# Sums of one-addend norms as transposes with VectorE adding columns, the last norm's spread in one bank, and the second input tile issued on ScalarE's queue

## The chip, the cores and the metric

The kernel runs on one core of one Trainium2 chip. The metric is device time in microseconds (us) of one execution; lower is better. Five engines work side by side and meet at semaphores: TensorE (PE in the profile; its weight loads are PEld), VectorE (DVE), ScalarE (ACT), GpSimd (POOL) and SyncE (SP), which here only issues DMAs. ScalarE issues some DMAs as well. Each engine works through its own list of instructions in order. Every queue of DMAs is served by the same 16 DMA engines.

## The reference

One encoder layer over 1024 tokens of width 1024, in float32:

```
hn   = rmsnorm(x, norm_mix)
proj = hn @ w_in                          # 1024 x 2304
o_a  = window_gqa_sink(qa, ka, va, sink)  # 8 query heads, 2 key heads, |i-j| <= 128, rotary
o_b  = neighbourhood_attention(qb, kb, vb, rpb)   # 8 heads, 2-D window 8 x 16, learned bias
mix  = concat(rmsnorm(o_a, norm_a), rmsnorm(o_b, norm_b))
h    = x + mix @ w_out
hn   = rmsnorm(h, norm_ffn)
h    = h + (silu(conv3(hn @ w_gate)) * (hn @ w_up)) @ w_down      # 1024 x 2816 between
out  = rmsnorm(h, norm_final)
```

with `rmsnorm(x, g) = x * rsqrt(mean(x * x) + 1e-6) * g`, the mean taken over the features of one token. There are five such norms.

## The kernel before

Activations are kept transposed: 128 features in the partitions, tokens along the row, so a tile is 128 x 1024 (or 128 x 512 for one half of the tokens). Every matrix product is float32 made of three passes: each operand is split into a rounded high part (ScalarE, a Copy) and the remainder (VectorE, a subtraction), and TensorE adds high x high, high x low and low x high into one PSUM bank (`block`, lines 167 to 170, and `group`, lines 881 to 885). PSUM has eight banks, taken under the tags pj, o, s and pt, two each.

The program runs in five stages: (1) the head, where the input x and the first three column tiles of w_in are loaded and split and six banks are filled (lines 85 to 164 and 576 to 660); (2) attention, with the remaining projections as filler between its steps (to line 826); (3) the end of w_out (lines 827 to 965); (4) the gated MLP's first half; (5) the product with w_down and the final norm (from line 1147). The order of TensorE's instructions is written out by hand (`manual_schedule`, line 127). The other engines' lists are put in order by a planner with its own model of costs; `pin` and `behind` fix some places in it. So an edit in one place can move instructions of other places in the lists of ScalarE, VectorE, GpSimd and SyncE.

*The head.* `load_x(k)` loads input tile k, `load_first_w(m, ks)` the k-tiles `ks` of column tile m (m = 0, 1, 2). SyncE issues x0's first half, then w at k = 0, w at k = 1, both halves of x1, w at k = 2 and 3, x2, x3, w at k = 4 to 7, x4 to x7; ScalarE issues the small parameters and x0's second half. `split_x` and `split_first_w` split them in the same order, and `add_square` adds up the squares of x over the eight tiles on VectorE. TensorE then goes over k, per k over two token halves and three column tiles. Behind the x tiles SyncE issues the constants, the rotary table, the next column tiles' weights (`fetch_w`, line 154, into `raw`, two buffers) and the tables of the learned bias (`bias_tiles`, line 435, into `rr`, one buffer). GpSimd builds a bias tile from `rr` (lines 443 and 444), and only then may the next `rr` be loaded. ScalarE and VectorE split `raw` (lines 160 and 161).

*A norm.* The squares are added over the feature tiles on VectorE until one 128 x 512 tile (the addend) stands for a token half; what is left is a sum over the partitions. `inverse_narrow` does this on TensorE: for each 128 tokens the addend is the stationary operand and a column of ones (each 1/1024) the moving one, which leaves one column of PSUM per 128 tokens (line 199); ScalarE takes the root (line 202), VectorE the reciprocal (line 203). `widen` then spreads the four columns over all partitions with four transposes of a broadcast column (line 210) into a bank. It is called twice in the head (addend `acc`), twice for norm_a (`narrow_a`, `wide_a`), twice for norm_b (`vb2`, line 843), once for each half of norm_ffn (lines 953 and 1099), and for the final norm once for the second token half (line 1368) and once for each quarter of the first half (lines 1385 and 1390), each with two addends `parts[..., 2]` and `parts[..., 3]`.

*The final norm.* `finish` (line 1299) calls `widen` twice, into two banks: one is read by VectorE, which scales six of the eight output tiles (line 1309), the other is copied to SBUF by ScalarE (line 1303), for GpSimd, which scales the other two (line 1307). Each tile's store is issued after it (line 1310), for the last quarter in turn by SyncE and ScalarE.

In the head TensorE's order is: the last k-tiles of column tile 0, four blocks with the two sums in their middle (line 646), two blocks of column tile 1, the two spreads (line 649), then two more blocks of column tile 1 and four of column tile 2. ScalarE copies the spread to `rstd1`, and VectorE multiplies the six banks with it (line 216).

Of the kernel before, what the change touches and what calls it, by code (L numbers as in the profile page):

```python
# [53 lines left out]
def hybrid_layer(tc, xT, w_in, w_out, w_gate, w_up, w_down, small, sink, rpb, consts, rope, out):  # L54
    nc = tc.nc
    with ExitStack() as ctx:
        pool = lambda name, bufs, **kw: ctx.enter_context(tc.tile_pool(name=name, bufs=bufs, **kw))
        cpool = pool("const", 1)
# [29 lines left out]
        def load_x(k, part=slice(0, S), queue=nc.sync):  # L88
            pin(queue.dma_start(xts[k][:, part], xT[k, :, part]))
# [11 lines left out]
        def load_first_w(m, ks):  # L101
            raw, at = head[ks.start // 4][m][0], slice(ks.start % 4, ks.start % 4 + ks.stop - ks.start)
            pin(nc.sync.dma_start(raw[:, at], w_in[m, :, ks, :]))

        steps = [slice(0, 1), slice(1, 2), slice(2, 4), slice(4, 8)]
        load_x(0, tsl(0))
        nc.scalar.dma_start(par[:, 0:C_SINK], small)
        load_x(0, tsl(1), nc.scalar)
        for m in range(3):
            load_first_w(m, steps[0])  # L110
        for m in range(3):
            load_first_w(m, steps[1])
        load_x(1, tsl(0))
        load_x(1, tsl(1))
        for m in range(3):
            load_first_w(m, steps[2])
        for k in (2, 3):
            load_x(k)
        for m in range(3):
            load_first_w(m, steps[3])  # L120
# [73 lines left out]
        def inverse_narrow(sqs, dim, tag, n=4):  # L194

            ps = bank("ss", tag)
            for i, sq in enumerate(sqs):
                for c in range(n):
                    nc.tensor.matmul(ps[:, c:c + 1], sq[:, c * 128:(c + 1) * 128], ones[:, 0:1], start=c == 0 and i == 0,
                                     stop=i == len(sqs) - 1, skip_group_check=True)  # L200
            v = cpool.tile([128, 4], F32, name="v4", tag="v4", bufs=4)
            nc.scalar.activation(v[:, 0:n], ps[:, 0:n], AF.Sqrt, bias=eps, scale=float(D) / dim)
            nc.vector.reciprocal(v[:, 0:n], v[:, 0:n])
            return v

        def widen(v, tag, n=4):

            wide = bank("sw", tag)
            for c in range(n):
                nc.tensor.transpose(wide[:, c * 128:(c + 1) * 128], v[:, c:c + 1].to_broadcast([128, 128]), ident)  # L210
            return wide
# [375 lines left out]
        def split_first_w(m, ks):  # L587
            raw, hi, lo = (t[:, ks.start % 4:ks.start % 4 + ks.stop - ks.start] for t in head[ks.start // 4][m])
            pin(nc.scalar.activation(hi, raw, AF.Copy))
            pin(nc.vector.tensor_tensor(lo, raw, f32(hi), op=ALU.subtract))  # L590
            first[m].w += [(hi[:, j], lo[:, j]) for j in range(ks.stop - ks.start)]

        def add_square(t, acc):
            s2 = tmp("sq")
            pin(nc.scalar.activation(s2, t, AF.Square))
            if acc is not None:
                pin(nc.vector.tensor_tensor(s2, s2, acc, op=ALU.add))
            return s2
# [10 lines left out]
            split_first_w(m, steps[1])  # L609
        for h in range(2):  # L610
            split_x(1, tsl(h))
        for m in range(3):
            split_first_w(m, steps[2])
        acc = add_square(xts[0], None)
        for k in range(2, KT):
            split_x(k)
            if k == 3:
                for m in range(3):
                    split_first_w(m, steps[3])
# [226 lines left out]
        for h in range(2):  # L846
            wide = widen(vb2[h], "pt")
# [96 lines left out]
        for h in range(2):  # L944
            for d in range(KT):
                if h == 0 and d + 2 < KT:
                    wo.append(load_wo(d + 2, fpool))
                ps = bank("pj", ("o", "s", "pj")[(h * KT + d) % 3])
# [3 lines left out]
                if h == 1 and d == 1:  # L952
                    v = inverse_narrow([total[0]], D, "pt")
# [5 lines left out]
                if h == 1 and d == 2:  # L959
                    wide = widen(v, "pt")  # L960
# [138 lines left out]
        v = inverse_narrow([total[1]], D, "pt")  # L1099
        units[1].p2()  # L1100
        wide = widen(v, "pt")
# [174 lines left out]
        sq, todo, vs = {}, [], {}  # L1276
# [21 lines left out]

        def finish(h, v, cols=whole, split=False):
            n = (cols.stop - cols.start) // 128  # L1300
            wide, again = widen(v, "pt", n), widen(v, "pt", n)
            copy = half("wide")
            nc.scalar.activation(copy[:, cols], again[:, 0:128 * n], AF.Copy)  # L1303
            for i, d in enumerate([d for d in range(KT) if d not in APART] + list(APART)):
                x = at_res(d, h, cols)
                if d in APART:
                    nc.gpsimd.tensor_tensor(x, x, copy[:, cols], op=ALU.mult)  # L1307
                else:
                    nc.vector.scalar_tensor_tensor(x, x, col(C_NFIN + d), wide[:, 0:128 * n], op0=ALU.mult, op1=ALU.mult)
                (nc.scalar if split and i % 2 else nc.sync).dma_start(out[d, :, h * HALF + cols.start:h * HALF + cols.stop], x)  # L1310
# [12 lines left out]
        def leave_quarter(j, ps, cols):  # L1323

            x = at_res(j + NP, 0, cols)
            add(j + NP, 0, ps, cols)
            s2 = parts[cols.start, j] = half("s2")[:, cols]
            nc.scalar.activation(s2, x, AF.Square)
            if j + NP < KT - 1:
                nc.vector.tensor_tensor(s2, s2, sq[0][:, cols], op=ALU.add)  # L1330

        tags = lambda j, y: ("s", "s", "pt", "pt")[j] if y else ("pj", "pj", "o", "o")[j]
        banks = {}
# [2 lines left out]
        for i, (p, j, c) in enumerate(order):  # L1336
# [4 lines left out]
            f, n = PARTS[c]  # L1341
# [4 lines left out]
            ps = banks[p, j]  # L1346
# [139 lines left out]
```

## Time and profile before

| | |
|---|---|
| Median of 3 runs | 1087.44 us (1087.1 to 1087.69) |
| Profiled execution | 1088.62 us |
| Its span, first to last instruction | 1086.8 us |
| Instructions | 14983 |
| Mean granted TensorE clock | 0.997 of full speed |
| Moved by DMA | 144.94 MB |

The profiled execution's own time stands 1.18 us above the median of the runs, and 1.8 us lie around its span. In the profile's rows `L199` is line 199 of the kernel before; a row of the timeline has start, duration, engine, line, operation, output <- inputs, shape and count, and in brackets how long the engine was idle before it and what released it. A float32 matmul with a one-column moving operand leaves two records.

### The profile page before, as it was taken

The numbers are of one execution on the slowest core, as the hardware profiler recorded it, in microseconds if no ns is written. First come the engines' busy times: TensorE is split into PE (matmuls) and PEld (weight loads), VectorE is DVE, ScalarE is ACT, GpSimd is POOL, SyncE is SP. The second block draws the span as 40 slices with busy tenths as digits, with TensorE's granted clock in tenths as the row PEclk, the third lists the DMA queues.
The fourth block names the chain that finished last, engine by engine and source line by source line (L and its number), as shares of the span: only waits on it lengthen the run. The fifth ranks groups of instructions, "written<-read, shape, count | busy, mean of one in ns | idle before, by whom it ended". The sixth has DMA issues, their size and how long they took to land.

```text
span 1086.8 us, 14983 instructions
## 1 busy us (share of the span) xinstructions
PE 1070.2 (98%) x5144; PEld 895.0 (82%) x5144; DVE 860.1 (79%) x1570; ACT 554.5 (51%) x1047; POOL 105.0 (10%) x188
## 2 busy tenths in 40 slices
PE   8999999999999999999999999999999999999997
PEld 7888888888888888887788888888888888888887
DVE  6789787667788688899998877877887867897764
ACT  7457676556676545545434334342433645444451
POOL 0223332222232100000000000000000000000001
PEclk9999999999999999999999999999999999999998
DMA  8223022232225147214342222323322788867644
GB/s 275 73 73 88 30 68 59 78 77 78 78 68 161 65 137 249 88 39 157 134 146 107 107 107 97 120 95 111 111 88 97 244 297 295 272 214 241 227 129 155
DMA packets 69084, 144.94 MB, mean 133 GB/s; under 512 B 8208, under 2 KB 19600, under 8 KB 69008
## 3 DMA queue, kind: packets, MB, share of 16 engines
q1 hardware_dynamic: 58784, 118.43, 34.6%
q10 hardware_dynamic: 10224, 25.56, 6.2%
q8 instruction: 40, 0.66, 0.3%
q14 instruction: 36, 0.29, 0.1%
HBM read 103.58 MB, written 28.57 MB: 122 GB/s over the span
## 4 chain that ended last, share of the span: by engine, by line
PE 88%; DVE 8%; ACT 2%; DMA 1%; issue 1%; SPq 0%; POOL 0%; DVEq 0%; ACTq 0%; POOLq 0%
PE pj L168 7%; PE pj L169 7%; PE pj L170 7%; PE dn L883 6%; PE dn L885 6%; PE dn L884 6%; PE z L885 5%; PE z L884 5%; PE z L883 5%; PE s L344 3%; PE x L883 3%; PE x L884 3%; PE x L885 3%; PE y L885 3%; PE y L884 3%; PE y L883 3%
## 5 line engine op out<-in xcount | busy, mean ns | idle before, releaser
L872 ACT ACTIVATE whi<-ws 128x512 fp32r<-128x512 f32 (+1 forms) x100 | 60.3, 623 | 127.8 <-DVE ws L990 80.5
L883 PE MATMUL dn<-xd,whi 128*128 128x512 f32 (+1 forms) x330 | 124.1, 376 | 0.0
L885 PE MATMUL dn<-xd,wlo 128*128 128x512 f32 (+1 forms) x330 | 123.7, 375 | 0.0
L884 PE MATMUL dn<-xd,whi 128*128 128x512 f32 (+1 forms) x330 | 123.7, 375 | 0.0
L168 PE MATMUL pj<-xgh,whi 128*128 128x512 f32 x248 | 104.4, 421 | 1.0 <-ACT xgh L584 1.0
L885 PE MATMUL z<-hg,wlo 128*128 128x512 f32 x264 | 103.0, 390 | 0.7 <-DVE wlo L873 0.7
L883 PE MATMUL z<-hg,whi 128*128 128x512 f32 x264 | 102.9, 390 | 0.0
L884 PE MATMUL z<-hg,whi 128*128 128x512 f32 x264 | 102.7, 389 | 0.0
L370 ACT ACTIVATE p<-p,nm 128x385 f32<-128x385 f32 (+3 forms) x128 | 75.1, 587 | 50.4 <-DVE nm L366 49.3
L169 PE MATMUL pj<-xgl,whi 128*128 128x512 f32 x248 | 97.5, 393 | 0.9 <-DVE xgl L585 0.8
L170 PE MATMUL pj<-xgh,wlo 128*128 128x512 f32 x248 | 97.6, 394 | 0.0
L374 POOL TENSOR_SCALAR p<-p,sm 128x384 f32<-128x384 f32 (+1 forms) x128 | 74.9, 598 | 219.3 <-DVE sm L372 204.7
L873 DVE TENSOR_TENSOR wlo<-raw,whi 128x512 fp32r<-128x512 f32 (+1 forms) x102 | 66.4, 671 | 26.6 <-ACT whi L872 26.4
L872 ACT ACTIVATE whi<-raw 128x512 fp32r<-128x512 f32 (+1 forms) x102 | 60.6, 612 | 45.2 <-DMA raw<-in_w_down_dram 20.0
L873 DVE TENSOR_TENSOR wlo<-ws,whi 128x512 fp32r<-128x512 f32 (+1 forms) x100 | 66.9, 681 | 21.0 <-ACT whi L872 20.8
L380 DVE TENSOR_TENSOR pl<-pt,ph 128x384 fp32r<-128x384 f32 (+2 forms) x108 | 63.3, 589 | 24.3 <-ACT ph L379 23.0
L1307 POOL TENSOR_TENSOR h<-h,wide 128x256 f32<-128x256 f32 (+1 forms) x6 | 5.4, 924 | 709.9 <-ACT wide L1303 709.9
L379 ACT ACTIVATE ph<-pt 128x384 fp32r<-128x384 f32 (+2 forms) x108 | 55.2, 514 | 32.2 <-PE pt L479 25.1
L885 PEld LDWEIGHTS dn<-xd,wlo 128*128 128x128 f32 x330 | 62.1, 188 | 11.3
L884 PEld LDWEIGHTS dn<-xd,whi 128*128 128x128 f32 x330 | 62.1, 188 | 11.1
L883 PEld LDWEIGHTS dn<-xd,whi 128*128 128x128 f32 x330 | 62.1, 188 | 11.1
L1198 ACT ACTIVATE xd<-xd 128x512 fp32r<-128x512 f32 x77 | 47.5, 626 | 44.0 <-DMA xd<-x 43.2
(220 smaller groups left out, 2671.2 us busy)
## 6 DMA issues: line engine op xcount, KB each, us to landing
xd<-x SPq DMA_DIRECT2D x77, 256.0 KB, 4.6
raw<-in_w_down_dram SPq DMA_DIRECT2D x72, 256.0 KB, 3.6
raw<-in_w_gate_dram SPq DMA_DIRECT2D x22, 512.0 KB, 3.4
raw<-in_w_up_dram SPq DMA_DIRECT2D x22, 512.0 KB, 3.8
x<-c ACTq DMA_DIRECT2D x22, 512.0 KB, 3.5
raw<-in_w_in_dram SPq DMA_DIRECT2D x30, 256.0 KB, 2.9
raw<-in_w_down_dram SPq DMA_DIRECT2D x36, 192.0 KB, 3.8
x<-t ACTq DMA_DIRECT2D x11, 512.0 KB, 2.6
```

Of the source, the lines that this page charges most:

```text
L168: nc.tensor.matmul(ps, w[0], x[0][:, tsl(h)], start=first, stop=False)
L169: nc.tensor.matmul(ps, w[0], x[1][:, tsl(h)], start=False, stop=False)
L170: nc.tensor.matmul(ps, w[1], x[0][:, tsl(h)], start=False, stop=last)
L370: nc.scalar.activation(p[:, j, 0:e], p[:, j, 0:e], AF.Exp, bias=nm, scale=-1.0, accum_out=sm[:, j:j + 1])
L374: nc.gpsimd.tensor_scalar(p[:, i, 0:m], p[:, i, 0:m], sm[:, i:i + 1], 1.0, op0=ALU.mult, op1=ALU.mult)
L379: nc.scalar.activation(ph[:, 0:n], ps[:, 0:n], AF.Copy)
L380: nc.vector.tensor_tensor(pl[:, 0:n], ps[:, 0:n], f32(ph[:, 0:n]), op=ALU.subtract)
L872: nc.scalar.activation(hi, src, AF.Copy)
L873: nc.vector.tensor_tensor(lo, src, f32(hi[:, :, :]), op=ALU.subtract)
L883: nc.tensor.matmul(ps, w[0], x[0], start=first and i == 0, stop=False, skip_group_check=True)
L884: nc.tensor.matmul(ps, w[0], x[1], start=False, stop=False, skip_group_check=True)
L885: nc.tensor.matmul(ps, w[1], x[0], start=False, stop=last and i == len(ws) - 1, skip_group_check=True)
```

## The change

Four edits:

1. `inverse_narrow` has two ways. With one addend, TensorE transposes it in 128-column pieces into a PSUM bank (one pass each, tokens now in the partitions), VectorE sums each piece along the row with one `tensor_reduce`, and the root reads its result from SBUF with the scale 1/dim. With two addends it is as before.
2. `finish` calls `widen` once, and VectorE and ScalarE read the same bank.
3. For the first quarter of the first token half, VectorE first adds `parts[0, 2]` to `parts[0, 3]`, so that the sum has one addend. The sum moves one group of matmuls later (from behind the group 1, 2, 0 to behind 1, 2, 1), and `finish` two groups later (from behind 1, 2, 1 to behind 1, 3, 0).
4. In the head, both halves of x1 are issued on ScalarE's queue, ahead of its first work, and w's k-tiles 1, 2 and 3 come in one load per column tile (128 x 384) in place of two (128 x 128 and 128 x 256).

```diff
-        steps = [slice(0, 1), slice(1, 2), slice(2, 4), slice(4, 8)]
+        steps = [slice(0, 1), slice(1, 4), slice(4, 8)]
         load_x(0, tsl(0))
         nc.scalar.dma_start(par[:, 0:C_SINK], small)
         load_x(0, tsl(1), nc.scalar)
+        load_x(1, tsl(0), nc.scalar)
+        load_x(1, tsl(1), nc.scalar)
         for m in range(3):
             load_first_w(m, steps[0])
         for m in range(3):
             load_first_w(m, steps[1])
-        load_x(1, tsl(0))
-        load_x(1, tsl(1))
-        for m in range(3):
-            load_first_w(m, steps[2])
...
             ps = bank("ss", tag)
-            for i, sq in enumerate(sqs):
+            v = cpool.tile([128, n], F32, name="v4", tag="v4", bufs=4, padded_shape=[128, 4])
+            if len(sqs) == 1:
                 for c in range(n):
-                    nc.tensor.matmul(ps[:, c:c + 1], sq[:, c * 128:(c + 1) * 128], ones[:, 0:1], ...)
-            nc.scalar.activation(v[:, 0:n], ps[:, 0:n], AF.Sqrt, bias=eps, scale=float(D) / dim)
+                    nc.tensor.transpose(ps[:, c * 128:(c + 1) * 128], sqs[0][:, c * 128:(c + 1) * 128], ident)
+                nc.vector.tensor_reduce(v, ps[:, 0:n * 128].rearrange("p (c w) -> p c w", w=128), axis=mybir.AxisListType.X, op=ALU.add)
+                nc.scalar.activation(v, v, AF.Sqrt, bias=eps, scale=1.0 / dim)
+            else:
+                ... (the lines removed above)
             nc.vector.reciprocal(v[:, 0:n], v[:, 0:n])
...
-            wide, again = widen(v, "pt", n), widen(v, "pt", n)
+            wide = widen(v, "pt", n)
             copy = half("wide")
-            nc.scalar.activation(copy[:, cols], again[:, 0:128 * n], AF.Copy)
+            nc.scalar.activation(copy[:, cols], wide[:, 0:128 * n], AF.Copy)
...
             if j + NP < KT - 1:
                 nc.vector.tensor_tensor(s2, s2, sq[0][:, cols], op=ALU.add)
+            elif cols.start == 0:
+                nc.vector.tensor_tensor(s2, s2, parts[0, j - 1], op=ALU.add)
...
-                    if (k, j, c) == (1, 2, 0):
-                        vs[0] = inverse_narrow([parts[0, 2], parts[0, 3]], D, "s", 2)
                     if (k, j, c) == (1, 2, 1):
+                        vs[0] = inverse_narrow([parts[0, 3]], D, "s", 2)
+                    if (k, j, c) == (1, 3, 0):
                         finish(0, vs[0], quarters[0])
```

In the compiled program the planner also moves other instructions. In the head, SyncE's list before had two loads of `rr`, two of `raw`, the third `rr`, one `raw`; now it has three loads of `rr` and then three of `raw`. ScalarE's split of the third `raw` stood behind the two roots and now stands ahead of them (and of their table load); VectorE's remainder of it stood behind the two reciprocals and now stands ahead of the two reduces. GpSimd builds the second bias tile ahead of its small copies of `nsink`, no longer behind five of them.

More of the change, by code (lines that the diff above doesn't have):

```diff
@@ L119, in hybrid_layer @@
         for m in range(3):
-            load_first_w(m, steps[3])
+            load_first_w(m, steps[2])
         for k in range(4, KT):
@@ L196, in inverse_narrow @@
             ps = bank("ss", tag)
-            for i, sq in enumerate(sqs):
+            v = cpool.tile([128, n], F32, name="v4", tag="v4", bufs=4, padded_shape=[128, 4])
+            if len(sqs) == 1:
                 for c in range(n):
[L199 to L202, printed above, removed]
+                    nc.tensor.transpose(ps[:, c * 128:(c + 1) * 128], sqs[0][:, c * 128:(c + 1) * 128], ident)
+                nc.vector.tensor_reduce(v, ps[:, 0:n * 128].rearrange("p (c w) -> p c w", w=128), axis=mybir.AxisListType.X, op=ALU.add)
+                nc.scalar.activation(v, v, AF.Sqrt, bias=eps, scale=1.0 / dim)
+            else:
+                for i, sq in enumerate(sqs):
+                    for c in range(n):
+                        nc.tensor.matmul(ps[:, c:c + 1], sq[:, c * 128:(c + 1) * 128], ones[:, 0:1], start=c == 0 and i == 0,
+                                         stop=i == len(sqs) - 1, skip_group_check=True)
+                nc.scalar.activation(v[:, 0:n], ps[:, 0:n], AF.Sqrt, bias=eps, scale=float(D) / dim)
             nc.vector.reciprocal(v[:, 0:n], v[:, 0:n])
@@ L611, in hybrid_layer @@
             split_x(1, tsl(h))
-        for m in range(3):
-            split_first_w(m, steps[2])
         acc = add_square(xts[0], None)
@@ L618, in hybrid_layer @@
                 for m in range(3):
-                    split_first_w(m, steps[3])
+                    split_first_w(m, steps[2])
             acc = add_square(xts[k - 1], acc)
```

## The prediction

> **What bounds the kernel now.** I read the page's busy times and the chain that ended last, then TensorE's waits over the whole span.
>
> ```profile
> span 1086.8 us, 14983 instructions
> PE 1070.2 (98%) x5144; PEld 895.0 (82%) x5144; DVE 860.1 (79%) x1570; ACT 554.5 (51%) x1047; POOL 105.0 (10%) x188
> PE 88%; DVE 8%; ACT 2%; DMA 1%; issue 1%; SPq 0%; POOL 0%; DVEq 0%; ACTq 0%; POOLq 0%
> ...
> PE pj L168 <- ACT xgh L584: 1.0, 1, 1.0
> PE pj L169 <- DVE xgl L585: 0.8, 1, 0.8
> ...
> PE sw L210 <- DVE v L203: 0.6, 1, 0.6
> PE ss L199 <- ACT s L1328: 0.6, 1, 0.6
> ```
>
> TensorE is busy 98% of the span and makes 88% of the chain. So whatever shortens its list counts in full, and so does every new wait in it. The four waits are those the change touches: 1.8 us at the second and third input tile (L168, L169), 0.6 before a spread of norm_b, 0.6 before the last sum.
>
> **The change part by part.** *TensorE's own work.* The groups by line and shape give the prices:
>
> ```profile
> L210 PE MATMUL sw<-cst,v 128*128 128x128 f32 x48 | 7.2, 281 | 1.3 <-ACT rstda L723 0.7 <-DVE v L203 0.6
> ...
> L199 PE MATMUL ss<-ones,sq 128*128 128x1 f32 x48 | 5.6, 247 | 0.0
> L199 PE MATMUL ss<-ones,s 128*128 128x1 f32 x40 | 4.9, 240 | 0.6 <-ACT s L1328 0.6
> ```
>
> Before there are 44 sums in 88 records: 10.5/44 = 0.24 us each. 48 transposes take 7.2 us, 0.15 each; the eight of the head, below, take 1.03 us, 0.13 each, and I use this one. 40 sums go (four of the last quarter stay) and 38 transposes come; 8 of the spreads' transposes go. 40 x 0.24 = 9.6 off, 38 x 0.13 = 4.9 on, 8 x 0.13 = 1.0 off: 5.7 us less, 0.9 of it in the head.
>
> *The head's sum and spread: a new wait.* Here are the timelines of GpSimd, SyncE, ScalarE, VectorE and TensorE, in this order, around the first norm.
>
> ```profile
> 27.25 1.93 POOL L443 TENSOR_TENSOR xb<-cst,rr 128x384 f32<-128x384 f32 x1 [26.27 <-DMA rr<-in_rpb_dram]
> 29.12 1.72 POOL L444 TENSOR_TENSOR xb<-cst,rr 128x256 f32<-128x256 f32 x1
> ...
> 34.82 0.98 POOL L443 TENSOR_TENSOR xb<-cst,rr 128x384 f32<-128x384 f32 x1
> 35.76 0.72 POOL L444 TENSOR_TENSOR xb<-cst,rr 128x256 f32<-128x256 f32 x1
> ...
> 30.87 0.55 SPq L435 DMA_DIRECT2D rr<-in_rpb_dram  x1
> 32.55 2.14 SPq L154 DMA_DIRECT2D raw<-in_w_in_dram  x2
> 36.50 0.55 SPq L435 DMA_DIRECT2D rr<-in_rpb_dram  x1
> 37.24 0.44 SPq L154 DMA_DIRECT2D raw<-in_w_in_dram  x1
> ...
> 29.95 1.28 ACT L202 ACT_TABLE_LOAD   x1
> ...
> 35.70 0.27 ACT L202 ACTIVATE v<-ss,eps 128x4 f32<-128x4 f32 x1 [0.63 <-PE ss L199]
> 35.86 0.62 ACT L160 ACTIVATE whi<-raw 128x512 fp32r<-128x512 f32 x1
> ...
> 35.99 0.18 DVE L203 RECIPROCAL v<-v 128x4 f32<-128x4 f32 x1 [0.72 <-ACT v L202]
> 36.51 0.70 DVE L161 TENSOR_TENSOR wlo<-raw,whi 128x512 fp32r<-128x512 f32 x1 [0.34 <-ACT whi L160]
> ...
> 38.37 1.03 PE L210 MATMUL sw<-cst,v 128*128 128x128 f32 x8
> 39.16 0.47 PE L168 MATMUL o<-xgh,h 128*128 128x512 f32 x1
> ```
>
> Each load of `rr` is issued 0.02 to 0.03 us after GpSimd is done with the one before (30.84 to 30.87, 36.48 to 36.50), since there is one buffer. Before, the third `raw` went out at 32.55, ahead of the third `rr`. In the changed program it stands behind it, and behind it stand, on ScalarE, its split, the table load and the roots, and on VectorE its remainder, the reduces and the reciprocals; TensorE's spread waits for these. So the first norm now hangs on GpSimd's second bias tile. The two loads' times from issue to landing are, for `rr` and for line 154:
>
> ```profile
> DMA to landing us min/median/max: 3.4/3.7/4.0
> ...
> DMA to landing us min/median/max: 2.6/2.9/4.5
> ```
>
> The new chain, on the clock of before: second `rr` issued 30.87, landed 34.3 (3.4); bias tile 1.66 (34.82 to 36.48; before, small copies stood ahead of it): 36.0; third `rr` issued, third `raw` 0.74 behind (36.50 to 37.24): 36.75; landed at 40.15 (I take 3.4, between median and maximum, as it queues behind `rr`); split 0.62, remainder 0.70, two reduces, root 0.27, reciprocal 0.18. No `tensor_reduce` is in this trace; the nearest row is VectorE reading a whole PSUM bank:
>
> ```profile
> 423.31 0.68 DVE L903 TENSOR_TENSOR h<-pj,h 128x512 f32<-128x512 f32 x1
> ```
>
> I take 0.68 each, with 0.55 and 1.9 (the slowed L443) as ends. With 0.25 for hand-overs the second reciprocal ends at 43.5; the table load (1.28) runs beside the remainder and the first reduce. Four transposes (0.52) and a hand-over later L168 starts at 44.2 in place of 39.16: +5.0 us. TensorE would be at the spread at about 36.2 (38.14 less 0.9 for the sums and about 1 of the input waits), so it stands idle some 6 us; its cheaper sums (0.9) and any gain in the input loads are inside this wait and bring nothing.
>
> *The input loads.* They move the chain's start, the first `rr`, which lands when the first burst of DMAs is through. Stretches of the head:
>
> ```profile
> 4.00:6.00 2.00, 1.91 (x9) 1.52 (x9) 1.24 (x4) 1.91 (x5) 0.00 (x0) 1.00 0.89 214
> 6.00:8.00 2.00, 2.00 (x11) 1.63 (x10) 1.47 (x5) 0.75 (x4) 0.00 (x0) 1.00 1.08 298
> 8.00:10.00 2.00, 2.00 (x10) 1.58 (x9) 1.13 (x2) 1.69 (x3) 0.00 (x0) 1.00 0.85 238
> ...
> 14.00:16.00 2.00, 0.51 (x1) 0.19 (x1) 1.24 (x2) 2.00 (x3) 0.00 (x0) 1.00 1.01 382
> ```
>
> The columns are the stretch, the busy times of TensorE, its loads, VectorE, ScalarE and GpSimd, the granted clock, the DMA engines' busy share and GB/s. From 4 to 10 us 214, 298 and 238 GB/s move against 382 later: 1.5 MB in 6 us that would take 3.9. Longer rows and x1 issued early cannot bring more than these 2.1; I take half, 1.1 (ends 0 and 2.1). [...] On ScalarE the two issues stand ahead of its first work:
>
> ```profile
> 1.18 0.46 ACTq L89 DMA_DIRECT2D xt<-in_xT_dram  x1
> ...
> ACT xgh L584 <- DMA par<-in_small_dram: 0.8, 1, 0.8
> ```
>
> They take 2 x 0.46, and ScalarE's first split waits 0.8 for its parameters anyway: 0.1 late at most. SyncE has five issues fewer ahead of x2. Without any gain the shift stays +5.0; with mine it is +3.9. Its ends are 2.1 (2.1 earlier, `raw` landing in 2.6) and 8.5 (no gain, 4.5, slow reduces).
>
> *TensorE's clock behind the wait.* Twice before TensorE falls still: in 14 to 16 us (above, 0.51 busy, clock 1.00), and at the end, among the last sums and spreads:
>
> ```profile
> 1080.00:1081.00 1.00, 0.81 (x4) 0.41 (x4) 0.57 (x2) 0.15 (x1) 0.00 (x0) 0.58 0.00 0
> ...
> 43.35 0.82 PE L297 MATMUL vt<-cst,t 128*128 128x128 f32 x6
> ```
>
> There the granted clock is 0.58. The longest wait before is about 1 us, so an idle of 6 us should do what the end does. How long it stays down is not shown; if all that lies between 39.16 and 43.35 ran at half the clock, it would cost 4.2 us more; if it came back at once, nothing. I take 2.0. [...]
>
> *The other norms.* Outside the head TensorE's list is 4.8 us shorter. Every sum now has a reduce on VectorE between transposes and root, and stands behind what VectorE has queued.
>
> ```profile
> 424.70 0.17 DVE L203 RECIPROCAL v<-v 128x4 f32<-128x4 f32 x1
> ...
> 426.76 0.60 PE L210 MATMUL sw<-cst,v 128*128 128x128 f32 x4
> ```
>
> For norm_ffn's first half the reciprocal moves behind a reduce, a remainder and one addition (3 x 0.68), from 424.70 to about 426.7, while the spread, at 426.76, would come 0.4 sooner: 0.7 lost. For norm_b, where the spread waited for the reciprocal already (0.6, above), two reduces eat the whole 0.9 that the sums give. For norm_a two more reduces ahead of a remainder that TensorE needs: 0.5. The second half of norm_ffn and the final norm's second half have slack. The last quarters: one addition and a reduce of 256 columns hide behind two groups of matmuls, but VectorE now waits for ScalarE's copy of the shared bank:
>
> ```profile
> 1080.42 2.44 DVE L1309 SCALAR_TENSOR_TENSOR h<-h,par,sw 128x256 f32<-128x256 f32 x6 [0.63 <-PE sw L210]
> ...
> 1080.85 0.38 ACT L1303 ACTIVATE wide<-sw 128x256 f32<-128x256 f32 x1 [1.26 <-PE sw L210]
> ```
>
> VectorE's six start 0.4 later; the copy, and with it GpSimd's two, 0.4 sooner: even at the very end, 0.4 lost in the quarter before. So 2.5 of 4.8 comes back: -2.3 (ends -4.8 and 0).
>
> Sum: 3.9 + 2.0 - 2.3 = +3.6 us. Against the profiled execution, 1088.62: 1092.2. The median of the runs, 1087.44, is 1.18 lower: **1091.0**.
>
> **The rivals.** *The wait is covered (faster).* If the third `raw` is there in time, the head gains: its 1.8 us of waits less 0.4 (an estimate: three splits of w of 384 columns in place of 128, 0.7 for 512, now stand ahead of x1's on each engine) and 0.9 of sums. Total -2.3 - 2.3 = -4.6: 1082.8. For this it must land by about 33: the spread is reached at 36.2, and 3.3 us of split, remainder, reduces, root and reciprocal lie between. That is 6 us sooner than my 39.0 (40.15 less 1.1). Against it speaks that the bias tile alone ended at 36.48.
>
> *It cancels.* The wait is there, the clock does not fall, and the other norms keep all they save: 3.9 - 4.8 = -0.9, or with 2.3 kept +1.6: 1086.5 to 1089.0, no measurable change (0.2% is about what the runs tell apart, 2.2 us). For it: in 14 to 16 us the clock holds.
>
> *VectorE becomes the bound.* It is at 79% and gets ten reduces (6.5 us). If those outside the head cost TensorE their full time, 5.2 us in place of 2.5, and the clock stays down for all 4.2: 3.9 + 4.2 - 4.8 + 5.2 = +8.5, 1095.9. Against it: TensorE waits little for VectorE before.
>
> **How the numbers follow.** The forecast has 0.57 (its own range 1088.0 to 1094.5), covered 0.15, cancelling 0.2, VectorE 0.08. Slower takes most of the first and the last: 0.63; faster the second and a little: 0.16; the same 0.21. The range 1083.0 to 1095.5 leaves out half of the second and of the last.
>
> **What would show it.** Right: in the head L210 starts at 42 or later, behind an idle TensorE of over 4 us, VectorE's remainder of the third `raw` ends just before the first reduce, and the granted clock in 42 to 46 us is under 1.00. Wrong: L210 before 38, or `raw` landing before 35. The input loads: the wait for xgh at the third tile is gone. The reduces: each 0.6 to 0.8 us.

## The result and the profile after

The changed kernel takes 1092.70 us (median of 6 runs, 1090.95 to 1093.61), the kernel before 1087.49 (6 runs): a ratio of 1.0045, with a 95% interval of 1.0033 to 1.0056. It is slower by 5.2 us. The profiled execution took 1092.49 us; its span is 3.9 us longer than before and not 5.2, since the profiled execution of before stood 1.1 us above its median and this one stands 0.2 below.

The page of the changed kernel, and TensorE's waits (who waited for whom: total, times, longest):

```profile
span 1090.7 us, 14891 instructions
PE 1067.5 (98%) x5094; PEld 890.5 (82%) x5094; DVE 867.2 (80%) x1578; ACT 554.7 (51%) x1044; POOL 105.2 (10%) x188
...
PE sw L214 <- DVE v L207: 5.6, 4, 4.5
PE pj L166 <- ACT whi L593: 0.5, 1, 0.5
```

TensorE's own work went down by 2.7 us (1070.2 to 1067.5) although part of it ran at a granted clock of 0.50 (below). One wait of 4.5 us came: the spread (L214) for VectorE's reciprocals (L207). The timelines of GpSimd, SyncE, ScalarE, VectorE and TensorE around it, of the changed kernel:

```profile
25.42 1.29 POOL L447 TENSOR_TENSOR xb<-cst,rr 128x384 f32<-128x384 f32 x1 [24.44 <-DMA rr<-in_rpb_dram]
31.97 1.28 POOL L447 TENSOR_TENSOR xb<-cst,rr 128x384 f32<-128x384 f32 x1 [3.58 <-DMA rr<-in_rpb_dram]
33.21 1.70 POOL L448 TENSOR_TENSOR xb<-cst,rr 128x256 f32<-128x256 f32 x1
...
28.42 7.06 SPq L439 DMA_DIRECT2D rr<-in_rpb_dram  x2
35.65 6.02 SPq L152 DMA_DIRECT2D raw<-in_w_in_dram  x3
...
39.96 0.63 ACT L158 ACTIVATE whi<-raw 128x512 fp32r<-128x512 f32 x1 [9.39 <-DMA raw<-in_w_in_dram]
40.61 1.28 ACT L200 ACT_TABLE_LOAD   x1
41.95 0.30 ACT L200 ACTIVATE v<-v,eps 128x4 f32<-128x4 f32 x1
...
40.62 0.69 DVE L159 TENSOR_TENSOR wlo<-raw,whi 128x512 fp32r<-128x512 f32 x1 [5.09 <-ACT whi L158]
41.23 1.28 DVE L199 TENSOR_REDUCE v<-ss 128x4 f32<-128x512 f32 x2
42.43 0.17 DVE L207 RECIPROCAL v<-v 128x4 f32<-128x4 f32 x1
42.88 0.18 DVE L207 RECIPROCAL v<-v 128x4 f32<-128x4 f32 x1 [0.28 <-ACT v L200]
...
34.51 1.04 PE L198 MATMUL ss<-cst,sq 128*128 128x128 f32 x8
37.90 0.39 PE L168 MATMUL o<-xgh,l 128*128 128x512 f32 x1
42.74 1.94 PE L214 MATMUL sw<-cst,v 128*128 128x128 f32 x8 [4.45 <-DVE v L207]
44.33 0.78 PE L166 MATMUL o<-xgh,h 128*128 128x512 f32 x1
47.89 0.59 PE L168 MATMUL s<-xgh,w 128*128 128x512 f32 x1
48.32 0.39 PE L166 MATMUL s<-xgh,w 128*128 128x512 f32 x1
```

Read it backwards. The spread's first four transposes wait for the first reciprocal (42.43 + 0.17 = 42.60), the other four for the second (42.88). The first reciprocal waits for ScalarE's root (41.95). Two things that the root needs end together just before it: the table load on ScalarE (40.61 + 1.28 = 41.89) and the first reduce on VectorE (41.23 + 0.64 = 41.87). The reduces stand behind the remainder of the third `raw` (40.62), and this waits for ScalarE's split (39.96), behind which the table load stands as well. The split waits for the DMA that SyncE issued at 35.65, right after GpSimd was done with the second bias tile (33.21 + 1.70 = 34.91) and the third `rr` had gone out.

TensorE stands still from 38.13 (one step of 0.23 after the last matmul's start at 37.90) to 42.74. What follows is slow: the eight transposes take 1.59 until L166 starts, where before they took 0.79, and nine matmuls come 0.43 us apart instead of 0.23, up to 48.32. The stretches of time show the clock (columns as in the prediction's stretches):

```profile
41.00:41.50 0.50, 0.00 (x0) 0.00 (x0) 0.50 (x2) 0.50 (x1) 0.00 (x0) 0.98 0.05 16
41.50:42.00 0.50, 0.00 (x0) 0.00 (x0) 0.50 (x2) 0.44 (x2) 0.00 (x0) 0.50 0.00 0
...
48.00:48.50 0.50, 0.50 (x3) 0.40 (x2) 0.00 (x0) 0.00 (x0) 0.00 (x0) 0.69 0.03 4
```

The granted clock fell to 0.50 at about 41.48 and came back to 1.00 at about 48.31 (a share of 0.98 or 0.69 in half a microsecond says where in it the step lies). The mean granted clock of all six runs is 0.994 to 0.996, against 0.997 in the profile of before, so the profiled run is no exception. From the first sum to the transposes of v, the next work after the six banks, it was 9.64 us before (33.71 to 43.35) and is 15.89 now (34.51 to 50.40). The 6.25 more are made of: sums 1.0 shorter, 4.6 idle, 0.8 for the spread at half clock, 1.84 for the nine matmuls.

### The profile page after: what moved, and what is told of

It reads as the page before. It is cut to its first block, busy times and chain, and to the rows that moved or that the text cites. A ratio compares the mean times of both kernels' runs of the same rounds, so it can differ in the third digit from the quotient of the medians.

```text
span 1090.7 us, 14891 instructions
## 1 busy us (share of the span) xinstructions
PE 1067.5 (98%) x5094; PEld 890.5 (82%) x5094; DVE 867.2 (80%) x1578; ACT 554.7 (51%) x1044; POOL 105.2 (10%) x188
## 3 DMA queue, kind: packets, MB, share of 16 engines
q1 hardware_dynamic: 58064, 117.90, 33.6%
## 4 chain that ended last, share of the span: by engine, by line
PE 82%; DVE 10%; ACT 3%; DMA 2%; issue 2%; POOL 0%; DVEq 0%; ACTq 0%; SPq 0%; POOLq 0%
PE dn L887 6%; PE dn L886 6%; PE dn L885 6%; PE pj L166 6%; PE pj L168 6%; PE pj L167 6%; PE z L887 5%; PE z L885 5%; PE z L886 5%; PE s L348 3%; PE x L885 3%; PE x L886 3%; PE x L887 3%; PE y L887 3%; PE y L885 3%; PE y L886 3%
## 5 line engine op out<-in xcount | busy, mean ns | idle before, releaser
L166 PE MATMUL pj<-xgh,whi 128*128 128x512 f32 x248 | 104.4, 421 | 1.5 <-ACT xgh L588 1.0
L1201 DVE TENSOR_TENSOR xd<-xd 128x512 fp32r<-128x512 f32 x77 | 52.1, 687 | 22.1 <-ACT xd L1200 21.7
```

Of the source, the lines that this page charges most:

```text
L166: nc.tensor.matmul(ps, w[0], x[0][:, tsl(h)], start=first, stop=False)
```

## The experiments

Each ratio is to the kernel before on the same chip, with its 95% interval; the medians of before were 1087.84 (runs 1 to 4), 1087.66 (5 to 8) and 1087.84 (9 to 12).

**1 and 2: take the wait away, in two ways.** The first moves one DMA, the second only the order on ScalarE and VectorE:

```diff
 # 1: bias_tiles(h)
-nc.sync.dma_start(raw, src)
+with tc.issue_after(fetched[2].ins) if h == 2 else ExitStack():     # fetched[2]: the load of the third raw
+    nc.sync.dma_start(raw, src)
...
 # 2: the split of the third raw, jobs[1].load()
-with behind(*["stack"] * (i == 1)):
+with behind(*["stack"] * (i == 1), *["root", "inverse"] * (i == 0)):
     jobs[i + 1].load()
```

> The changed kernel with one DMA moved: the load of the third bias row (rr) is held behind the third raw on SyncE's queue, as it was before the change; nothing else moves on any engine. Theory 1 (the first norm hangs on the second bias tile through the third raw): raw is issued as soon as its buffer is free, about 32.4, lands about 35.8; its split, remainder and the two reduces still stand ahead of the roots, so the spread starts at about 39.0 instead of 42.74, TensorE waits about 1 us instead of 4.6, and the granted clock stays at 1.00. 3.6 of the wait and 2.6 of the clock come back: 1092.7 - 6.2 = 1086.5. Rival A (the reduces on VectorE hold the spread whatever raw does): spread at 42 or later, 1091 or more. Rival B (the head's time is given back further on, since VectorE or the weights are what the next stage waits for): the spread comes early but the time stays above 1089.

> The changed kernel with the load order left as it is (third rr ahead of third raw on SyncE), but the split of the third raw on ScalarE and its remainder on VectorE are put behind the first norm's roots and reciprocals. Theory 1: raw lands at about 39.9 as in the changed kernel, but nothing that the spread needs stands behind it. Reduces at about 35.5 to 36.8, second reciprocal at about 37.3, so the spread starts where TensorE's list reaches it, about 38.1, with no wait and no loss of clock: 4.6 + 2.6 come back, 1092.7 - 7.2 = 1085.5. The late split costs nothing, since its product comes some 15 us later. Rival A (the reduces hold the spread): spread at 40 or later, 1089 or more. Rival B (given back later): the spread at 38 but the time above 1089.

Measured: 1085.38 (ratio 0.9976, 0.9966 to 0.9985) and 1085.36 (0.9976, 0.9967 to 0.9986). First SyncE, ScalarE and TensorE of run 1, then ScalarE, VectorE and TensorE of run 2:

```profile
31.54 0.34 SPq L152 DMA_DIRECT2D raw<-in_w_in_dram  x1
34.33 0.63 ACT L158 ACTIVATE whi<-raw 128x512 fp32r<-128x512 f32 x1 [6.00 <-DMA raw<-in_w_in_dram]
37.16 1.04 PE L214 MATMUL sw<-cst,v 128*128 128x128 f32 x8
```

```profile
38.91 0.63 ACT L158 ACTIVATE whi<-raw 128x512 fp32r<-128x512 f32 x1 [2.78 <-DMA raw<-in_w_in_dram]
34.52 1.27 DVE L199 TENSOR_REDUCE v<-ss 128x4 f32<-128x512 f32 x2
37.20 1.03 PE L214 MATMUL sw<-cst,v 128*128 128x128 f32 x8
```

In both, the spread starts where TensorE's list reaches it, with no wait and at full clock; the first sum to v's transposes takes 8.6 us. In run 2 `raw` comes as late as in the changed kernel (split 5.3 us after the first sum began, there 5.5), and nothing waits for it. So the reduces do not hold the spread, the late `raw` ahead of reduces and roots does, and what is won is not given back: 7.3 us in the medians, as against 7.2 expected of run 2. Run 1 came out 1.1 below its expectation: `raw` was there at 34.33 and not at 35.8, and the 1 us of wait that I had left in did not occur.

**3, 4 and 9: which edit moves the DMA.** Run 3 is the kernel before with edit 4 (the input loads) alone, run 4 the changed kernel without it, run 9 is run 3 with the `rr` held back as in run 1:

```diff
 # 3 and 9, against before; 4 leaves this out of the changed kernel
-steps = [slice(0, 1), slice(1, 2), slice(2, 4), slice(4, 8)]
+steps = [slice(0, 1), slice(1, 4), slice(4, 8)]
...
+load_x(1, tsl(0), nc.scalar)
+load_x(1, tsl(1), nc.scalar)
...
```

> The kernel before with the input loads of the change alone (second input tile on ScalarE's queue, w in steps of 1, 3 and 4); sums, spreads and the last norm as before. In this program too the third rr goes out ahead of the third raw, and ScalarE splits that raw ahead of the roots. Theory 1: raw lands at about 39.9, split 0.6, table load 1.3, roots, reciprocals: spread at about 42.7 against 38.37 before, 4.3 later, with the old sums; clock lost for 0 to 2.6 us, as the idle is about 3.5 us: 1091.8 to 1094.4, slower. So the loss belongs to the input loads and not to the sums. Rival A (the reduces make the wait): no wait here, and with some gain from the loads 1086 to 1088.5.

> The changed kernel with the input loads of the kernel before; all the sums as transposes with reduces, one bank for the last norm's spread. Theory 1: the third raw goes out ahead of the third rr and lands at about 35.8; it is split ahead of the roots, so the spread starts at about 38.7 against 38.37 before, the clock stays at 1.00, and what the other norms save remains, about 3: 1087.5 + 0.3 - 3.1 = 1084.7. Rival A (the reduces hold the spread in any case): 1089 or more. Rival B (what the other norms seemed to save was the shift of something else): 1087 to 1088.

> The kernel before with the input loads of the change, and the third rr held behind the third raw on SyncE as it was: the loads without the wait that they bring. Theory 1 now: the loads make the new order of the queue and nothing else; in the profiles so far the first norm's sum starts at 33.55, 33.58, 34.51 and 32.83 with them and at 33.71 and 32.90 without, so they bring nothing that can be told from the spread of the runs: 1087.2 to 1088.2, as before. Rival (my prediction's case of a covered wait): TensorE's 1.8 of waits for the second and third input tile go, 1.4 net: 1086.3. Rival (the wider splits cost more): 1088.5 or more.

Measured: run 3 1093.54 (1.0051, 1.0038 to 1.0064), run 4 1084.88 (0.9975, 0.9965 to 0.9985), run 9 1087.82 (1.0001, 0.9993 to 1.0010). Run 3, ScalarE and TensorE, with the old sums and no reduce in it:

```profile
39.29 0.63 ACT L158 ACTIVATE whi<-raw 128x512 fp32r<-128x512 f32 x1 [11.40 <-DMA raw<-in_w_in_dram]
39.94 1.28 ACT L200 ACT_TABLE_LOAD   x1
32.83 1.84 PE L197 MATMUL ss<-ones,sq 128*128 128x1 f32 x16
41.76 1.97 PE L208 MATMUL sw<-cst,v 128*128 128x128 f32 x8 [4.26 <-DVE v L201]
```

The same wait without any reduce: the table load behind the split ends at 39.94 + 1.28 = 41.22, and root and reciprocal follow it. So the new order of SyncE's queue comes from the input loads alone: with them the planner puts three `rr` before the third `raw`, without them two. On ScalarE `raw` is split ahead of the roots in run 3 and in run 4; in run 4 it lands in time (split at 34.63) and the spread waits 0.5. With the order restored by hand (run 9) the loads bring no gain: that rival (1086.3, a ratio of 0.9986) lies outside the interval. The rival of a loss (1088.5, a ratio of 1.0006) lies inside it, so a loss of up to about 1 us is not ruled out.

**5 and 6: keep TensorE at work in the wait.** The four transposes of the second token half come last before the spread, done six times, or are preceded by 16 matmuls with the identity:

```diff
-for c in range(n):
+for c in list(range(n)) * times:                                # run 5; run 6 puts nc.tensor.matmul(..., ident)
     nc.tensor.transpose(...)                                    # in such a loop, ahead of the four transposes
...
-vs1 = [inverse_narrow([acc[:, tsl(i)]], D, "pt") for i in range(2)]
+vs1 = [inverse_narrow([acc[:, tsl(0)]], D, "pt")]
 if p is first[1] and h == 0:
+    vs1.append(inverse_narrow([acc[:, tsl(1)]], D, "pt", times=6))      # run 6: times=4
```

> The changed kernel with the four transposes of the first norm's second half moved to just ahead of the spread in TensorE's list and done six times over (the same values into the same bank): 24 transposes, about 3.1 us, that fill TensorE's idle time from 37.6 to about 40.9 and end before VectorE comes to the second reduce. The wait for the reciprocals stays (spread at about 42.7). If the lost clock is the price of the idle and transposes keep the clock up: granted clock 1.00 after the spread, 2.6 us less than the changed kernel, 1090.1. Rival A (transposes do not count as work for the clock): the clock falls as before, 1092 to 1093. Rival B (the nine slow matmuls are slow for another reason than idle time): 1092 to 1093 too, whatever fills the wait.

> As the run with transposes in the wait, but with 16 ordinary matmuls of the squares with the identity (about 3.3 to 3.9 us; the four transposes follow them and write the bank last). If idle time alone lets the clock fall: clock 1.00 after the spread, 1090.1. If transposes do not count for the clock but matmuls do, this run is 2.6 us below the run with transposes; if both count, the two agree within 0.5 us. Rival B (the slow matmuls have another reason): both at 1092 to 1093.

Measured: 1092.95 (1.0048, 1.0035 to 1.0060) and 1092.88 (1.0042, 1.0029 to 1.0056), so no gain, and the two agree. TensorE and the clock in run 5, then in run 6:

```profile
36.37 2.78 PE L198 MATMUL ss<-cst,sq 128*128 128x128 f32 x24
41.23 0.62 PE L214 MATMUL sw<-cst,v 128*128 128x128 f32 x4 [2.07 <-DVE v L207]
43.44 0.62 PE L214 MATMUL sw<-cst,v 128*128 128x128 f32 x4 [1.59 <-DVE v L207]
...
43.00:44.00 1.00, 0.56 (x5) 0.59 (x6) 0.86 (x3) 0.00 (x0) 0.00 (x0) 1.00 0.00 0
44.00:45.00 1.00, 1.00 (x4) 0.78 (x3) 0.28 (x1) 0.60 (x1) 0.00 (x0) 0.51 0.00 0
47.00:48.00 1.00, 1.00 (x4) 0.79 (x4) 0.28 (x1) 0.00 (x0) 0.00 (x0) 0.79 0.00 0
```

```profile
39.83 0.60 PE L200 MATMUL ss<-cst,sq 128*128 128x128 f32 x4
41.12 0.62 PE L216 MATMUL sw<-cst,v 128*128 128x128 f32 x4 [0.69 <-DVE v L209]
43.33 1.09 PE L216 MATMUL sw<-cst,v 128*128 128x128 f32 x4 [1.59 <-DVE v L209]
...
43.00:44.00 1.00, 0.67 (x4) 0.70 (x5) 0.76 (x3) 0.00 (x0) 0.00 (x0) 0.66 0.00 0
46.00:47.00 1.00, 1.00 (x5) 0.78 (x4) 0.04 (x1) 0.00 (x0) 0.00 (x0) 0.63 0.00 0
```

The expectation failed, but the runs do not show that idle time is innocent. With the later transposes the second reduce moved behind the first reciprocal, and the second reciprocal behind the first evacuation, so the spread came in two halves with a wait before each, and in that thinned-out stretch the clock fell all the same, only later and for half as long: from 44.0 to 47.4 in run 5, 43.3 to 46.7 in run 6, against 6.8 us. What was saved of the clock went to the second wait: 16.5 and 16.4 us from the first sum to v's transposes, 15.9 in the changed kernel. The price of the clock alone is therefore not measured by an edit; it is read from the spacing of the matmuls.

**7 and 8: the sums alone, the last norm alone.** Run 7 is the kernel before with the new `inverse_narrow` (edit 1) alone, run 8 with the last norm's edits (2 and 3) alone:

```diff
 # 7
+nc.tensor.transpose(ps[:, c * 128:(c + 1) * 128], sqs[0][:, c * 128:(c + 1) * 128], ident)
+nc.vector.tensor_reduce(v, ...)
...
 # 8
-wide, again = widen(v, "pt", n), widen(v, "pt", n)
+wide = widen(v, "pt", n)
...
+nc.vector.tensor_tensor(s2, s2, parts[0, j - 1], op=ALU.add)
...
```

> The kernel before with the sums of one-addend norms alone as transposes with a reduce; input loads and the last norm's spread as before. Theory 1: the sums themselves cost nothing in the head (spread at about 37.3 to 38.7, wait 0.5 or less) and save nearly what TensorE's list gives outside it, 28 sums times 0.11, about 2.5 of 3.1 with small new waits for the reduces: 1087.8 - 2.4 = 1085.4. Rival A (the reduces cost VectorE's full time, 0.64 each): 1087 to 1090.

> The kernel before with the last norm's edits alone (one bank for the spread, the first quarter's sum with one addend made by an addition): 8 spread transposes (1.0) and 2 sums (0.5) fewer on TensorE, of which 0.5 lie beside the stores at the very end; against it VectorE's scaling behind ScalarE's copy, 0.3 in the quarter before (its add is held) and 0.4 at the end. Theory 1: 1087.8 - 1.0 + 0.7 = 1087.5, no measurable change. Rival (the shared bank costs more than it saves): 1088.5 or more. Rival (the list counts in full): 1086.5.

Measured: 1086.32 (0.9986, 0.9977 to 0.9995) and 1087.65 (1.0000, 0.9992 to 1.0009). The sums alone gain 1.3 us, half of what I expected; the last norm's edits gain nothing, as expected. The head of run 7 takes 9.6 us, as before: the 1.0 that its sums save goes into the roots, which stand behind the split of the third `raw`. TensorE's waits of run 7 show this and the other spreads that wait for reciprocals (0.6 in all before):

```profile
PE sw L216 <- DVE v L209: 2.4, 4, 0.9
```

By the timeline the four are 0.55 in the head, 0.24 at norm_b, 0.93 at norm_ffn's first half and 0.65 before the last quarter's spread. The last one is the 0.6 of the kernel before (0.64 at 1079.94); the other three are new.

**10, 11 and 12: the parts without the wait.** Run 10 is run 4 with the split behind the roots as in run 2. Run 11 is run 10 with two banks for the last norm's spread. Run 12 is run 11 with the input loads of the change.

```diff
 # 11 and 12
-wide = widen(v, "pt", n)
+wide, again = widen(v, "pt", n), widen(v, "pt", n)
```

> The changed kernel with the input loads of before, and with the split of the third raw behind the first norm's roots and reciprocals as in the second experiment: both causes of the wait are gone. Theory 1: the 0.51 that the spread still waited in the run without the loads goes: 1084.9 - 0.5 = 1084.4. Rival (the roots were not what the spread waited for there): 1084.9 or more.

> As the run before, with the last norm's spread in two banks again (8 transposes more), so that VectorE's scaling no longer stands behind ScalarE's copy. Theory 1: the end gets 0.6 shorter (0.3 in the quarter before, 0.4 at the very end), TensorE's list 0.8 longer, of which 0.1 is at the end already counted: the same within 0.5, 1084.4. Rival (the shared bank is the better one, since the list counts in full): 1085.2. Rival (the end counts in full and the transposes hide): 1083.7.

> As the run before, with the input loads of the change; the split of the third raw stays behind the roots, so no wait can come of them. Theory 1: the loads bring nothing: within 0.5 of the run before, 1084.4. Rival (they save the waits for the input tiles, 1.4): 1083.0. Rival (they cost something in the head apart from the wait, as the 0.8 by which the changed kernel's first sum came later): 1085.2.

Measured: 1084.80 (0.9974, 0.9963 to 0.9985), 1084.30 (0.9968, 0.9955 to 0.9980), 1084.58 (0.9970, 0.9958 to 0.9981). All three beat both kernels; among themselves and against run 4 the runs do not tell them apart. In run 10's profile the spread's wait is gone (8.6 us in the head, 9.6 in run 4), but its median is only 0.08 lower; why the microsecond does not show there stays open. At the end of the program the bank can be seen; first run 2 (one bank), then run 11 (two), the last quarter on VectorE, TensorE and ScalarE:

```profile
1074.45 0.42 DVE L1285 TENSOR_TENSOR h<-dn,h 128x256 f32<-128x256 f32 x1
1076.62 0.40 PE L214 MATMUL sw<-cst,v 128*128 128x128 f32 x2 [0.64 <-DVE v L207]
1077.06 0.39 ACT L1305 ACTIVATE wide<-sw 128x256 f32<-128x256 f32 x1 [0.78 <-PE sw L214]
1077.48 2.44 DVE L1311 SCALAR_TENSOR_TENSOR h<-h,par,sw 128x256 f32<-128x256 f32 x6 [1.00 <-ACT wide L1305]
```

```profile
1072.92 0.42 DVE L1289 TENSOR_TENSOR h<-dn,h 128x256 f32<-128x256 f32 x1 [0.29 <-PE dn L891]
1075.09 0.62 PE L216 MATMUL sw<-cst,v 128*128 128x128 f32 x4 [0.65 <-DVE v L209]
1075.54 2.44 DVE L1315 SCALAR_TENSOR_TENSOR h<-h,par,sw 128x256 f32<-128x256 f32 x6 [0.59 <-PE sw L216]
```

With one bank VectorE scales 0.86 us after the spread began, behind ScalarE's copy, with two 0.45. And its last addition, which began 0.20 after the last sum's matmuls (1072.72) with two banks, begins 0.53 after them (1073.92) with one.

**All profiles together.** From the first and last times of the sums, spreads and transposes of v in each profile (us):

| profile | first sum at | to v's transposes | to norm_ffn's first sum | to the end |
|---|---|---|---|---|
| before | 33.7 | 9.6 | 379.7 | 663.7 |
| changed | 34.5 | 15.9 | 378.2 | 662.1 |
| 1, 2 | 33.6, 33.6 | 8.6, 8.6 | 378.5, 379.1 | 663.9, 662.5 |
| 3 | 32.8 | 16.1 | 379.5 | 663.2 |
| 4 | 32.9 | 9.6 | 378.4 | 662.2 |
| 5, 6 | 33.2, 33.1 | 16.5, 16.4 | 378.5, 379.3 | 663.1, 662.3 |
| 7 | 33.5 | 9.6 | 378.4 | 663.3 |
| 8 | 35.3 | 9.5 | 379.7 | 663.1 |
| 9 | 33.6 | 9.5 | 379.8 | 663.7 |
| 10, 11, 12 | 32.3, 32.9, 33.1 | 8.6, 8.6, 8.6 | 378.2, 378.2, 378.7 | 662.5, 662.0, 662.0 |

The first sum starts at 33.4 on the mean with the new loads (8 profiles) and at 33.4 without (6), anywhere from 32.3 to 35.3. Run 8's 35.3 has a cause of its own, a fall of the clock from 16.3 to 19.7 us (below); without run 8 the mean without the loads is 33.1. From v's transposes to norm_ffn the four profiles with the old sums take 379.7, the ten with the new ones 378.6 on the mean: 1.1 us won. From there to the end, 663.5 with all the old parts (before, 3, 9), 662.7 with the new sums and one bank (7 profiles, 662.1 to 663.9), 662.0 in runs 11 and 12, with the new sums, edit 3 and two banks. Run 7, with the new sums and the last norm left as it was, takes 663.3, and run 8 takes 663.1. The seven profiles with one bank differ by 1.8 among themselves, so the table shows a gain of about 0.9 for all that is new here (662.6 on the mean of the ten profiles with the new sums), but not that two banks beat one.

## Why the prediction was right, point by point

The forecast was 1091.0, slower, with a range of its own of 1088.0 to 1094.5; measured 1092.7. The mechanism was the one described, and every sign named for it is there: the spread at 42.74, TensorE idle for over 4 us ahead of it, the remainder of the third `raw` just before the first reduce, the clock under 1.00 from 42 to 46 us. That the sum came so near is in part luck, as the terms show.

*The new wait.* It went link by link as written: third `rr` ahead of third `raw`, `raw` ahead of reduces and roots, spread behind them. Issue of `raw` predicted at 35.65 (36.75 less 1.1), measured 35.65, but by two errors that cancel: the second `rr` was there 1.2 sooner (31.97 against 33.2), and the bias tile took 2.94 instead of 1.66. That they cancel is luck. The landing took 4.3 and not 3.4 (39.96 against 39.05). From landing to second reciprocal 3.1 against 3.35. Reduces 0.64 each against 0.68. Counted from the first sum and without the clock, the wait is worth 4.6 - 1.0 = +3.6. The prediction counted to the matmul behind the spread: 44.33 less 39.16 is 5.2, and less 0.8 for the spread at half clock +4.4, since the first sum itself came 0.8 later (34.51 against 33.71); the sum had +3.9. What the prediction did not see is which edit causes it: it treated it as a matter of the head's sum and spread. Runs 3 and 4 put it on the input loads, and the sums need no wait at all (run 2).

*The clock.* Predicted +2.0 with ends 0 and 4.2, measured +2.64 (0.8 on the spread, 1.84 behind it). The clock stayed down for 6.83 us (below), 5.57 of them with TensorE at work (42.74 to 48.31).

*The input loads.* The step from the loads to the start of the chain holds: I gave them 1.1 us on the first `rr`, and GpSimd's first bias tile, which waits for it, starts at 24.7 on the mean of the 8 profiles with the new loads (23.8 to 25.4) and at 26.6 without (6 profiles, 26.0 to 27.3), so 1.8 sooner. What failed is the expectation that TensorE gains by it. I put the 1.8 us of waits before at the second and third input tile, but in the timeline both stand at the third (14.78 and 16.10). They are gone, as I said they would be. In their place the changed kernel has waits for w at the start (0.5, in the page above, and 0.3) and this one at the second tile:

```profile
12.05 0.49 PE L166 MATMUL pj<-xgh,whi 128*128 128x512 f32 x1 [0.99 <-ACT xgh L588]
```

ScalarE splits x1 there behind the third of the longer loads of w, for which it had waited 1.43 us (its split starts at 10.86). The first sum starts no sooner on the mean, and run 9 measures 1.0001. The 1.8 us on `rr` came with the second issuing queue and with longer loads together, and no run parts the two.

*TensorE's list and the other norms.* Predicted -2.3 of -4.8; measured -3.1 in the profile of the changed kernel (378.2 and 662.1 against 379.7 and 663.7), -2.0 on the mean of all profiles (-1.1 and -0.9). So the changed kernel's profile gives back a third (1.7 of 4.8) and the mean a little more than half, as the term had it. Where it is given back fits only in part. In the changed kernel norm_b's spread waits 0.24 and norm_ffn's 0.30, the last sum 0.32 longer (0.94 against 0.62), and VectorE's last scaling starts 0.4 later: 1.3 of the 1.7. The 0.9 that I took off for norm_b rested on a wrong reading: the wait of 0.6 for a reciprocal stands at 1079.94, before the last quarter's spread, and no spread of norm_b waited before. A line of the waits has no place in time; look it up in the timeline before you build on it.

*The last norm.* I wrote "even at the very end, 0.4 lost in the quarter before". The loss of 0.3 in the quarter before is right; at the very end it is not even but 0.4 worse, since VectorE's six tiles set the end and not GpSimd's two (in run 2 VectorE ends at 1077.48 + 2.44 = 1079.92, GpSimd at 1078.93).

*The median.* I took 1.18 off because the profiled execution of before stood that much above its median. That of the changed kernel stands 0.2 below its own. The sum was +3.6 and the two spans differ by 3.9; the medians differ by 5.2. In the spans the terms are +4.4 (wait), +2.6 (clock) and -3.1 (the rest) against +3.9, +2.0 and -2.3: misses of +0.5, +0.6 and -0.8 that nearly cancel. So the 1.7 by which the forecast was too low comes mostly from this step.

*The rivals.* The covered wait did not happen, but runs 1, 2 and 12 show what it is worth: 1085.4 to 1084.6 and not 1082.8, since the input loads bring TensorE nothing and the other norms 2.0. Cancelling failed on the clock. VectorE as the bound failed outside the head: TensorE gained there.

## What to carry to other kernels

When a planner orders the queues, ask of every edit which loads it moves past each other: here fewer and longer DMAs at the start, with no gain of their own that the runs show, put a load that hangs on GpSimd ahead of one that a norm hangs on, and that cost 7 us against the same edits with one order restored. Look for what stands in an engine's list ahead of the short chain that TensorE waits for (root, reduce, reciprocal), and put work that is needed some 15 us later behind it (run 2). Price a long wait on TensorE with the lower clock behind it: here a granted 0.50 behind a wait of 4.6 us, over half as much again (2.6 us).

## What the runs showed of the hardware that I had not expected

*The clock was down for 3.4 us or for twice that.* It was down for 6.83 us in the changed kernel (41.48 to 48.31) and 6.82 in run 3 (39.50 to 46.32), for 3.40 in run 5 (44.02 to 47.42), 3.42 in run 6 (43.32 to 46.74) and 3.42 in run 8 (16.26 to 19.68), worked out from the granted shares of such stretches. Work alone did not bring it back at once: in the changed kernel TensorE was at work from 42.74 on, and the granted clock was 0.50 for 5.57 us more. At the end of the changed kernel the clock fell again, at 1085.96:

```profile
1085.00:1086.00 1.00, 0.00 (x0) 0.00 (x0) 1.00 (x4) 0.00 (x0) 0.85 (x2) 0.98 0.00 0
```

That is 2.02 us after the end of TensorE's last row (1083.54 + 0.40); in the head it fell 3.19 us after the end of the last row before the wait (37.90 + 0.39).

What a wait costs can differ between executions. Run 8 and the kernel before have nearly the same two waits at the third input tile (0.79 and 0.82, 0.95 and 0.82), and the clock fell in run 8 alone. There the last 3.41 us before the fall (12.85 to 16.26) held 1.80 us of work; in the kernel before the same stretch held 1.64, and the granted clock was 1.00 from 12 to 20 us. What decides between the two is not shown. Run 8's profiled execution stood 1.7 above its median.

TensorE need not have been idle throughout the last 3.41 us before a fall. In run 6 they held 1.14 us of transposes, with gaps of 0.69 and 1.59 us, and in run 8 1.80 us of work. A threshold in busy time is not shown: before the fall at the end of the kernel before, at 1080.16, the same length held 2.14 us, one-column sums among them.

*The clock held through transposes.* In run 5 TensorE did nothing but float32 transposes from 36.37 to 39.15 and then stood still until 41.23, 4.86 us in all; the granted clock was 1.00 all the while and fell only at 44.02. In run 6, with ordinary matmuls from 36.26 and transposes behind them, it fell at 43.32.

*GpSimd's bias tile and VectorE's additions took longer side by side.* First the two operations of the second bias tile in run 1. Then, in the changed kernel, VectorE's addition of squares before GpSimd's second tile, and the next one beside it (the tile's own rows there, 31.97 and 33.21, are shown above):

```profile
33.48 0.98 POOL L448 TENSOR_TENSOR xb<-cst,rr 128x384 f32<-128x384 f32 x1 [3.70 <-DMA rr<-in_rpb_dram]
34.42 0.72 POOL L449 TENSOR_TENSOR xb<-cst,rr 128x256 f32<-128x256 f32 x1
```

```profile
30.59 1.21 DVE L601 TENSOR_TENSOR sq<-sq 128x1024 f32<-128x1024 f32 x1
32.33 2.00 DVE L601 TENSOR_TENSOR sq<-sq 128x1024 f32<-128x1024 f32 x1
```

The bias tile took 1.66 us in run 1, and 1.66 in the kernel before with VectorE busy for 0.36 of them (34.82 to 36.48); it took 2.94 (31.97 to 34.91) in the changed kernel with VectorE busy throughout, 2.00 of them with the addition of squares, and this addition took 2.00 instead of 1.21. The prediction's 1.66 was taken from the quiet row, and the tile was to move into the busy stretch.

*A load right behind `rr` landed late.* `raw` took 4.2 to 4.3 us from issue to split in the changed kernel and in runs 2 and 3 (35.65 to 39.96, 34.71 to 38.91, 35.01 to 39.29), 2.8 ahead of `rr` in run 1 (31.54 to 34.33). That the transfer of `rr` is what it waits for was not tried.
